# Conditioning weights of the first feed-forward asked for in threes from ScalarE, and the last layer's first weight sums for gate and up made at the end of attention

## The chip, the core and the metric

The kernel runs on one core of one Trainium2 chip. The core's engines each work through a queue of their own in order: TensorE (PE; its weight loads are shown as PEld), VectorE (DVE), ScalarE (ACT), GpSimd (POOL), and SP, which only issues transfers. ScalarE and GpSimd issue transfers too, from their own queues. Engines wait for one another through semaphores. The metric is the time of one execution in microseconds, as the median of several; lower is better.

## What is computed

Two layers of a diffusion backbone over 1024 latent tokens and 256 context tokens of width 1024. The parts that matter here:

```python
def swiglu(u, w_gate, w_up, w_down):
    return (jax.nn.silu(u @ w_gate) * (u @ w_up)) @ w_down

for i in range(DEPTH):                                  # two layers
    sh1, sc1, g1, sh2, sc2, g2 = ada_mod(c, ada_w[i], ada_b[i])   # silu(c) @ ada_w[i] + ada_b[i], in six
    u_lat = modulate(rms_norm(h_lat, norm1_g[i]), sh1, sc1)
    ...
    y_lat = mixer(...)         # layer 0: Fourier and Hyena; layer 1: neighbourhood attention, then @ na_w_out
    h_lat = h_lat + g1 * y_lat
    h_lat = h_lat + g2 * swiglu(modulate(rms_norm(h_lat, norm2_g[i]), sh2, sc2),
                                ffn_w_gate[i], ffn_w_up[i], ffn_w_down[i])
    # layer 0 does the same for the context tokens, with ada_mod(c_ctx, ...)
return rms_norm(h_lat, final_g)
```

The feed-forward's inner width is 2816, 22 blocks of 128. `ada_w` of a layer is 1024 x 6144, 48 blocks of 128 columns, 512 KB each.

## The kernel before

Values are carried transposed: 128 channels on the partitions, tokens along the free axis, eight blocks for the width of 1024. Products keep the accuracy of float32 by splitting each operand into a high part (made by ScalarE) and a low part (made by VectorE, which subtracts), and adding three products: high x high, high x low, low x high.

**The feed-forward's pair loop** (`ffn`, loop over `i`, 11 turns) makes gate and up for two blocks of the inner width at a time, with Winograd's scheme of seven products of half size in place of eight. `wino_weights` reads two weight rows of 512 KB (`ws` tiles, four buffers) and makes from their halves A11, A12, A21, A22 the sums S1 to S4 on VectorE (L1959 to L1967), then splits S1 to S4 and A22 into float16 high and low halves (`split_scaled`: L1840 on ScalarE, L1841 on VectorE; an `hl` tile is the split first row A11, A12). `wino_steps` runs the products on TensorE (L1981). Four of the seven accumulate in one PSUM bank, and between them the running sum is copied out by ScalarE (`snap`, L1986), so the next product on that bank waits for the copy; VectorE adds other banks to the copies (L1995, L2005, L2010). The gate's results then go through SiLU on ScalarE (L2125, L2127), VectorE multiplies them with up's (L2082) and makes further sums (L2085 to L2088), and GpSimd writes these out for the down projection (L338). One turn is 168 matmuls (2 x 7 products of 12). The scheduler of the framework fixes each engine's order when the program is built; `follow(x)` holds an instruction behind `x` on x's engine.

Beside the products a turn of layer 0 carries three more kinds of work:

- `ada_group`: the modulation vectors that are still missing (the last sixth of layer 0, all of layer 1) are sums over rows of `ada_w` blocks: GpSimd loads a block of 512 KB into an `s4` tile (L338), and VectorE multiplies it with the conditioning vector and sums, in two halves and for up to two conditioning vectors (L565; each shows as a CUSTOM_DVE and a short READ_ACCUMULATOR). Three blocks in each turn up to the eighth, two in the last three, 30 in all; the other 26 follow in the down projection.
- `scan`: sums of the absolute values of all gate and up rows of layer 1, for their scale. ScalarE loads a row itself (L335) and sums it some steps later (L1809); four `s4` tiles go round, four rows a turn.
- `sums`: combinations of w_down rows, loaded by SP, summed by VectorE (L2042 to L2045), written out by GpSimd.

The `s4` pool has 21 buffers. In the pair loop of layer 0 two hold the conditioning vectors, 14 the split operands, four the scan; one is left for the `ada_w` block.

**The way into the second feed-forward.** Attention (layer 1) works in groups of heads; its low halves of the transposed probabilities are made at L2530. Its TensorE time is filled with steps of the output projection over the heads already done: `first_part(0)` yields one step at a time. After it come `last_part(0)`, `first_part(1)` (its weight split is L351 on ScalarE and L353 on VectorE), and between them the first operands of the feed-forward (`wino_first`, L1775 to L1778). Behind `first_part(1)` stands `drain(self.wino_pair(1, 0, 0, sums, self.G))`: S1 to S4 and A22 of the first gate pair, from four half rows in `g` tiles. Then the first two products of several pairs are begun (`wino_begin`), and `ffn` starts: `wino_second` makes the other operands (L1853 scaling and splitting on ScalarE, L1854 and L1882 to L1903 on VectorE), while the first up pair's S1 to S4 and A22, and both of the second pair's, are made from `ws` rows among them.

Of the kernel before, what the change touches and what calls it, by code (L numbers as in the profile page):

```python
# [10 lines left out]
F32 = mybir.dt.float32  # L11
F32R = mybir.dt.float32r
F16 = mybir.dt.float16
AF = mybir.ActivationFunctionType
ALU = mybir.AluOpType
AX = mybir.AxisListType.X
MUL, ADD, SUB, MAX, MIN = ALU.mult, ALU.add, ALU.subtract, ALU.max, ALU.min

P = 128
# [239 lines left out]
class Builder:  # L259
# [280 lines left out]
    def ada_group(self, l, m, conds, where):  # L540

        nc, a = self.nc, self.a

        def load(nb):
            if where == "ws":
                t = self.W("ws", "ws")
                self.ld(t, a["ada_w"][l, nb])
                return [t[:, :512], t[:, 512:]]
            t = self.mat(1024, F32) if where == "mat" else self.S4()
            (self.ld if where == "mat" else self.ldr)(t, a["ada_w"][l, nb])  # L550
            return [t[:, :512], t[:, 512:]]

        ahead = l == 0 and m < 5
        ready = [load(m * 8)] if ahead else []
        for nb in range(m * 8, m * 8 + 8):
            if not ahead or nb < m * 8 + 7:
                ready.append(load(nb + len(ready)))
            st = ready.pop(0)
            for c in reversed(conds):
                half = self.pt.tile([P, 2], F32, tag="ah", name=self.nm("ah"))  # L560
                init = self.adab[:, l * 48 + nb:l * 48 + nb + 1]
                for j in (0, 1):
                    o = st[j] if c == 0 else self.T()
                    to = self.ada[(l, c)][:, nb:nb + 1] if j else half[:, 0:1]
                    nc.vector.tensor_tensor_reduce(o, st[j], self.cond[c][j], 1.0, init, MUL, ADD, to)  # L565
                    init = to
            yield
        sl = slice(m * 8, m * 8 + 8)
        for c in conds:
            t = self.ada[(l, c)]  # L570
            if m in (1, 4):
                g = (0 if m == 1 else 2) + l
                nc.vector.scalar_tensor_tensor(t[:, sl], t[:, sl], 1.0, self.gs[:, g * 8:g * 8 + 8], op0=ADD, op1=MUL)

    def late_groups(self, ms, where):

# [1222 lines left out]
    def scan(self, key, tiles):  # L1799

        nc = self.nc
        n = len(tiles)
        sums = self.C(2 * n)
        st = [self.S4() for _ in range(4)]
        for k in range(n + 4):
            t = st[k % 4]
            with self.follow(self.last_hi):
                if k > 3:
                    nc.scalar.activation(t, t, AF.Abs, accum_out=sums[:, k - 4:k - 3])  # L1809
                if k < n:  # L1810
                    self.lda(t, tiles[k])
            yield
        self.wsc[key] = sums
# [30 lines left out]
    def wino_second(self, h, l, m, r):  # L1844

        nc = self.nc
# [4 lines left out]
        def out(key, j, src):  # L1851
            hi, lo = self.pair((key, j), l == 1 or len(self.X) < 17)
            nc.scalar.copy(hi, src)  # L1853
            los.append(nc.vector.tensor_tensor(lo, src, self.raw_part(hi), SUB).ins)  # L1854

        los = []

# [169 lines left out]
    def ffn(self, l, u, h, hs, second, after, keep=None, begun={}):  # L2027

        nc, a = self.nc, self.a
# [19 lines left out]
        todo = iter(())  # L2049
        if l == 0:  # L2050
            self.pad(self.pt, PAD_T)
        if u is not None:
            wsums = self.wsc["here"] = self.C(4 * NFB)
            for fb in range(NFB):
                wide = 3 if fb < NFB - 2 else 2
                gh, gl = self.weights(a["gate"][l, fb], wide=wide, sums=wsums[:, fb:fb + 1])
                uh, ul = self.weights(a["up"][l, fb], wide=wide, sums=wsums[:, NFB + fb:NFB + fb + 1])
                lo = self.last_lo
                ga = self.lin(gh, gl, 0, range(KB), u, (2,))[2]
                ua = self.lin(uh, ul, 0, range(KB), u, (2,))[2]  # L2060
                t = self.T()
                nc.scalar.activation(t[:, :256], ga[:, :256], AF.Silu)
                nc.vector.tensor_tensor(t[:, :256], ua[:, :256], t[:, :256], MUL)
                self.ldr(hidc[fb // 2][:, fb % 2], t[:, :256])
                if fb >= 2:
                    with self.follow(last):
                        next(second, None)
                last = lo
            self.scale_w("here", [(0, 0), (0, 1)])
            self.load_cond(act=False)  # L2070
            todo = (x for l1, m in [(0, 5)] + [(1, m) for m in range(6)]
                    for x in self.ada_group(l1, m, (0, 1) if l1 == 0 or m < 2 else (0,), "s4"))

        ahead = iter(())
        if l == 0:
# [17 lines left out]
        for i in range(NFB // 2):  # L2093
            g, up = begun.get((i, 0)), begun.get((i, 1))
            if g is None or not g.whole:
                wg = self.wino_pair(l, i, 0, g and g.w)
                w = next(wg)
                next(wg)
            if g is None:
                g = Steps(self.wino_steps(w, lambda: self.either(self.G)))  # L2100
                g.to(1)
            if prev is not None:
                prev[0].to(7)
                finish(i - 1, prev[1])
            wu = self.wino_pair(l, i, 1, up and up.w)
            w = next(wu)
            if up is None:
                up = Steps(self.wino_steps(w, lambda: self.either(self.TK)))
            if i == 0:
                for k, _ in enumerate(second):  # L2110
                    if k == 11:
                        next(wu)
            next(wu, None)
            for k in (3, 4, 5) if i == 0 and l == 1 else ():
                g.to(k)
                up.to(k)
            next(ahead, None)
            g.to(5)
            up.to(1)
# [6 lines left out]
            t = self.G()  # L2126
# [9 lines left out]
            if i == 0 and u is not None:  # L2136
                with self.follow(self.last_hi):
                    for t in self.cond:
                        for x in t:
                            nc.scalar.activation(x, x, AF.Silu)  # L2140
            for _ in range(3 if i < 8 else 2):
                next(todo, None)
        for _ in ahead:
            pass
# [448 lines left out]
    def run(self):  # L2593
        nc, a = self.nc, self.a
# [9 lines left out]
        def drain(g):  # L2604
            for _ in g:
                pass
# [162 lines left out]
        h2, o, h4 = Act(), Act(), Act()  # L2769
# [19 lines left out]
        def by_row(x):  # L2789
            return x.rearrange("p (h r c) -> p r h c", r=8, h=4)  # L2790

        def first_part(pc):
            for nb in range(KB):
                with self.follow(self.last_mul if pc and nb > 1 else None):
                    wh, wl = self.weights(a["w_out2"][nb, :, :768], 768, load=None if pc else self.ldr)
                acc = self.PQ() if pc == 0 else self.PS()
                for kb in range(6):
                    if pc == 0 and nb == 0:
                        load_o(kb, (0,), self.ld)
# [28 lines left out]
        for i, _ in enumerate(first_part(1)):  # L2828
            if i == 7:
                c = self.rms_begin(0)  # L2830
            if i == 12:
                first = self.wino_first(h2, 1, 3, self.rms_end(0, c))
            if i > 12 and i % 3 == 1:
                with self.follow(self.last_lo):
                    next(first, None)
        sums = {}
        drain(self.wino_pair(1, 0, 0, sums, self.G))
        last_part(1)
        spill(h2, hs1, (1,))

# [45 lines left out]
        c = self.rms_begin(1)  # L2886
        begun[(0, 1)] = self.wino_begin(1, 0, 1, self.TK)
        r1 = self.rms_end(1, c)
        begun[(0, 0)].w.update(sums)
        begun[(0, 0)].whole = True  # L2890
        begun[(1, 0)] = self.wino_begin(1, 1, 0, self.G, self.TK)
        begun[(1, 1)] = self.wino_begin(1, 1, 1, self.TK, self.S2)
        begun[(2, 0)] = self.wino_begin(1, 2, 0, self.G, self.S2)
# [80 lines left out]
```

## Time and profile before

| | |
|---|---|
| median of 3 runs | 2902.62 us (2897.42 to 2906.07) |
| profiled execution, own time | 2895.03 us |
| its span, first to last instruction | 2892.9 us |
| mean granted TensorE clock | 0.983 |
| pair loop of layer 0 | about 908 to 1336 us |
| attention's last groups of heads | about 2085 to 2185 us |
| way into the second feed-forward | about 2185 to 2350 us |

The profile is of one execution. A row of a group of waits reads: who waited, at which line, for whom; total us, number of waits, the longest. A row of the timeline reads: start, duration, engine, line, operation, output<-input, shapes, how many were merged, and in brackets how long the engine had been idle and what ended that. Tile names drop their numbers: `s` is any tile of the two large pools (`s4`, `s2`), `ps` and `pq` are PSUM banks, `c` constants. "SPq" and "ACTq" rows are transfers being issued.

### The profile page before, as it was taken

The page shows a single profiled execution, that of the slowest core. Times are in us where ns is not written, and L with a number is a line of the kernel's source. Part 1 is how long each engine was busy: PE and PEld are TensorE (multiplying, and loading weights), DVE is VectorE, ACT ScalarE, POOL GpSimd, SP SyncE. Part 2 cuts the span into 40 slices and gives each one's busy share as a digit, 9 for nine tenths or more (in the row PEclk, how much of TensorE's full clock was granted, in tenths as well). Part 3 has the DMA queues.
Part 4 walks back from the last instruction along what each step waited for, and adds up shares of the span by engine and source line. Part 5 has one row for each costly group of instructions (what it writes and reads, how often), then busy time and mean ns, then how long its engine had stood idle before and what let it go on. Part 6 is the DMA issues. An engine that isn't in the chain of part 4 may idle for free. (4 is left out here: it accounts for less than half of the span.)

```text
span 2892.9 us, 43698 instructions
## 1 busy us (share of the span) xinstructions
PE 2752.6 (95%) x15570; PEld 1999.5 (69%) x15570; DVE 2095.6 (72%) x3683; ACT 1430.1 (49%) x2445; POOL 543.3 (19%) x877
## 2 busy tenths in 40 slices
PE   7999788999999999999999999999999999999998
PEld 3877677788897444445888988888887444444887
DVE  5678788768686887786887526777777976775556
ACT  3434235543686443454445426777764643343434
POOL 1210234341101112113020002333221012222000
PEclk9999999999999999999999999999999999999999
DMA  7355546656655666788995435877875235665664
GB/s 261 107 163 178 166 131 196 233 174 229 227 166 193 239 228 242 248 293 292 332 308 185 158 113 147 197 184 195 190 236 199 100 131 201 228 202 195 233 193 135
DMA packets 304936, 580.42 MB, mean 201 GB/s; under 512 B 82760, under 2 KB 129546, under 8 KB 304718
## 3 DMA queue, kind: packets, MB, share of 16 engines
q1 hardware_dynamic: 234894, 367.34, 40.7%
q0 software_dynamic: 60640, 182.50, 18.4%
q10 hardware_dynamic: 9184, 27.79, 2.8%
q8 instruction: 123, 2.02, 0.3%
q14 instruction: 95, 0.78, 0.1%
HBM read 430.17 MB, written 119.80 MB: 190 GB/s over the span
## 5 line engine op out<-in xcount | busy, mean ns | idle before, releaser
L1981 PE MATMUL ps<-s,s 128*128 128x512 f16 x2280 | 520.8, 384 | 29.1 <-ACT tk L1986 18.2
L1981 PEld LDWEIGHTS <-s 128*128 128x128 f16 x2640 | 260.3, 99 | 356.4 <-issue 50.3
L347 PE MATMUL ps<-s,wh 128*128 128x256 f32 (+1 forms) x1784 | 412.8, 334 | 8.3 <-ACT wh L351 5.2
L347 PEld LDWEIGHTS ps<-s,wh 128*128 128x128 f32 x1784 | 299.9, 191 | 43.5 <-ACT wh L351 6.9
L347 PE MATMUL ps<-s,wl 128*128 128x256 f32 (+1 forms) x892 | 272.9, 332 | 4.8 <-DVE wl L353 4.8
L351 ACT CAST s<-s 128x1024 fp32r<-128x1024 f32 (+2 forms) x192 | 172.9, 926 | 210.5 <-DMA s<-d 192.5
L2175 PE MATMUL ps<-s,s 128*128 128x512 f32 (+1 forms) x1000 | 259.0, 384 | 3.4 <-DVE s L353 3.2
L347 PE MATMUL pq<-s,wh 128*128 128x512 f32 (+1 forms) x840 | 255.8, 384 | 0.8 <-DVE s L901 0.5
L353 DVE TENSOR_TENSOR s<-s,s 128x1024 fp32r<-128x1024 f32 (+2 forms) x170 | 190.7, 1154 | 78.1 <-ACT s L351 77.7
L347 PE MATMUL ps<-s,s 128*128 128x65 f16 (+4 forms) x2748 | 229.4, 235 | 18.3 <-DMA s<-tk 9.9
L338 POOL DMA_DIRECT2D d<-s x245 | 133.6, 546 | 429.0 <-DVE s L1699 86.1
L1981 PE MATMUL ps<-s,hl 128*128 128x512 f16 x924 | 212.5, 379 | 1.2 <-ACT hl L1840 1.2
L2175 PEld LDWEIGHTS ps<-s,s 128*128 128x128 f32 x1000 | 184.3, 188 | 42.2 <-DVE s L353 5.7
L353 DVE TENSOR_TENSOR wl<-ws,wh 128x1024 fp32r<-128x1024 f32 (+1 forms) x102 | 121.3, 1192 | 120.6 <-ACT wh L351 116.1
L1981 PEld LDWEIGHTS <-hl 128*128 128x128 f16 x1056 | 103.2, 98 | 125.9 <-ACT hl L1840 1.4
L351 ACT CAST wh<-ws 128x1024 fp32r<-128x1024 f32 (+1 forms) x102 | 103.5, 1017 | 169.9 <-PE ps L347 89.9
L347 PEld LDWEIGHTS ps<-s,wl 128*128 128x128 f32 x892 | 166.3, 190 | 23.4 <-DVE wl L353 6.5
L347 PEld LDWEIGHTS pq<-s,wh 128*128 128x128 f32 x840 | 149.6, 189 | 23.0 <-ACT wh L351 1.1
L347 PE MATMUL pq<-s,wl 128*128 128x512 f32 (+1 forms) x420 | 159.1, 379 | 0.0
L2175 PE MATMUL ps<-s 128*128 128x512 f32 (+1 forms) x500 | 150.0, 386 | 1.6 <-DVE g L2010 1.6
L347 PEld LDWEIGHTS ps<-s,s 128*128 128x128 f32 (+1 forms) x828 | 130.4, 193 | 25.1 <-DVE s L353 2.6
L1840 ACT ACTIVATE s<-t,c 128x512 f16<-128x512 f32 x176 | 117.3, 712 | 23.8 <-DVE t L1964 9.9
(521 smaller groups left out, 5367.0 us busy)
## 6 DMA issues: line engine op xcount, KB each, us to landing
s<-d SPq DMA_DIRECT2D x283, 256.0 KB, 4.0
d<-s POOLq DMA_DIRECT2D x229, 256.0 KB, 3.6
s<-in_down SPq DMA_DIRECT2D x150, 256.0 KB, 6.2
s<-in_ada_w POOLq DMA_DIRECT2D x64, 512.0 KB, 5.6
ws<-in_up SPq DMA_DIRECT2D x44, 512.0 KB, 4.3
ws<-in_gate SPq DMA_DIRECT2D x42, 512.0 KB, 4.0
d<-s SPq DMA_DIRECT2D x60, 256.0 KB, 2.3
d<-g POOLq DMA_DIRECT2D x56, 256.0 KB, 3.6
```

Of the source, the lines that this page charges most:

```text
L338: self.last_ldr = self.nc.gpsimd.dma_start(out, in_).ins
L347: self.last_mm = self.nc.tensor.matmul(o, l, r, start=st, stop=sp).ins
L351: self.last_hi = nc.scalar.copy(hi, src).ins
L353: self.last_lo = eng.tensor_tensor(lo, src, hi.bitcast(F32), SUB).ins
L1840: self.last_hi = self.nc.scalar.activation(hi, src, AF.Copy, scale=s).ins
L1981: nc.tensor.matmul(ps, x[:, sl], y, start=first and j == 0 and x is wh and y is xh, stop=j == 3 and x is wl, skip_group_check=True)
L2175: m = nc.tensor.matmul(acc[j][:, c0:c1], x[:, sl], y[:, xs], start=first and k == 0, stop=last and k == 2, skip_group_check=True)
```

## The change

1. `ada_group` is replaced, in the pair loop of layer 0, by `ada_stream`. It takes three `s4` tiles of its own, has ScalarE issue three loads in a row (behind the last high half, `last_hi`), and sums the three blocks behind the last low half (`last_lo`). In turn 0 loads and sums stand at the end; in turns 1 to 9 the loads stand ahead of the scan's steps and the sums at the end. 30 blocks as before; the other 26 go on as before through GpSimd.
2. `scan` has two tiles in place of four.
3. The sums S1 to S4 and A22 of the last layer's first pair, for gate and for up, are made inside `first_part(0)`, before the third and the fifth of its eight blocks, from half rows that SP loads into `s2` tiles. The gate's `drain` behind `first_part(1)` and the up's work in the first turn of `ffn` are gone.
4. In layer 1 the second pair's weights are made behind the last low half of an operand that `wino_second` has made (`last_x`).

```diff
+    def ada_stream(self, groups, n):
+
+        blocks = [(l, m, m * 8 + k, conds) for l, m, conds in groups for k in range(8)]
...
+        own = [self.S4() for _ in range(3)]
+        for k in range(0, n, 3):
+            with self.follow(self.last_hi):
+                for t, b in zip(own, blocks[k:k + 3]):
+                    self.lda(t, self.a["ada_w"][b[0], b[2]])
+            yield
+            with self.follow(self.last_lo):
+                for t, b in zip(own, blocks[k:k + 3]):
+                    step(b, t)
+            yield
+        for b in blocks[n:]:
+            t = self.S4()
+            self.ldr(t, self.a["ada_w"][b[0], b[2]])
+            step(b, t)
+            yield
@@ scan
-        st = [self.S4() for _ in range(4)]
-        for k in range(n + 4):
-            t = st[k % 4]
+        st = [self.S4() for _ in range(2)]
+        for k in range(n + 2):
+            t = st[k % 2]
             with self.follow(self.last_hi):
-                if k > 3:
-                    nc.scalar.activation(t, t, AF.Abs, accum_out=sums[:, k - 4:k - 3])
+                if k > 1:
+                    nc.scalar.activation(t, t, AF.Abs, accum_out=sums[:, k - 2:k - 1])
@@ wino_second
             los.append(nc.vector.tensor_tensor(lo, src, self.raw_part(hi), SUB).ins)
+            self.last_x = los[-1]
@@ ffn
-            todo = (x for l1, m in [(0, 5)] + [(1, m) for m in range(6)]
-                    for x in self.ada_group(l1, m, (0, 1) if l1 == 0 or m < 2 else (0,), "s4"))
+            todo = self.ada_stream([(l1, m, (0, 1) if l1 == 0 or m < 2 else (0,))
+                                    for l1, m in [(0, 5)] + [(1, m) for m in range(6)]], 30)
...
-                w = next(wg)
-                next(wg)
+                with self.follow(self.last_x if l and i == 1 else None):
+                    w = next(wg)
+                    next(wg)
...
-            wu = self.wino_pair(l, i, 1, up and up.w)
-            w = next(wu)
-            if up is None:
-                up = Steps(self.wino_steps(w, lambda: self.either(self.TK)))
+            wu = iter(())
+            if up is None or not up.whole:
+                wu = self.wino_pair(l, i, 1, up and up.w)
...
-            next(wu, None)
+            with self.follow(self.last_x if l and i == 1 else None):
+                next(wu, None)
...
+            if i and i < 10:
+                next(todo, None)
             next(ahead, None)
...
+                next(todo, None)
-            for _ in range(3 if i < 8 else 2):
+            if i < 10:
                 next(todo, None)
@@ run
+        early = {}, {}
...
                 acc = self.PQ() if pc == 0 else self.PS()
+                if pc == 0 and nb in (2, 4):
+                    drain(self.wino_pair(1, 0, nb // 2 - 1, early[nb // 2 - 1], self.S2))
...
-        sums = {}
-        drain(self.wino_pair(1, 0, 0, sums, self.G))
...
-        begun[(0, 0)].w.update(sums)
-        begun[(0, 0)].whole = True
+        for m, x in enumerate(early):
+            begun[(0, m)].w.update(x)
+            begun[(0, m)].whole = True
```

How the instructions stand at the three places that matter. The lines of the changed program are its own: L1843 is the scan's sum (L1809 before), L1874 and L1875 the high and low halves (L1840, L1841), L2021 the copies out of PSUM (L1986), L2166 the SiLU (L2125), L570 the sums over `ada_w` (L565), L2045, L2030 and L2117 are L2010, L1995 and L2082, L1994 to L2002 are L1959 to L1967, L2572 is L2530, L2551 is L2509, L2548 is L2506.

ScalarE in a middle turn of layer 0's pair loop, before: the last split of up, four sums of the scan, the four loads of its next rows.

```order
L1840 ACTIVATE s_2617_10540<-t_10531,c_9148 128x512
L1809 ACTIVATE s_2390_9235,c_9234<-s_2390_9235 128x1024
L1809 ACTIVATE s_2391_9236,c_9234<-s_2391_9236 128x1024
L1809 ACTIVATE s_2392_9237,c_9234<-s_2392_9237 128x1024
L1809 ACTIVATE s_2393_9238,c_9234<-s_2393_9238 128x1024
L335 DMA s_2390_9235<-in_gate 128x1024
L1840 ACTIVATE hl_10843<-ws_10839,c_9148 128x1024
L1986 COPY g_10584<-ps_10458 128x512
L335 DMA s_2391_9236<-in_gate 128x1024
L335 DMA s_2392_9237<-in_gate 128x1024
```

The same engine and place in the changed program:

```order
L335 DMA s_2407_9420<-in_ada_w 128x1024
L335 DMA s_2408_9421<-in_ada_w 128x1024
L335 DMA s_2409_9422<-in_ada_w 128x1024
L1843 ACTIVATE s_2390_9235,c_9234<-s_2390_9235 128x1024
L1843 ACTIVATE s_2391_9236,c_9234<-s_2391_9236 128x1024
L1874 ACTIVATE hl_11154<-ws_11150,c_9148 128x1024
L335 DMA s_2390_9235<-in_gate 128x1024
L2166 ACTIVATE s_2647_10785<-s_2647_10785,c_9143 128x512
L335 DMA s_2391_9236<-in_gate 128x1024
L1843 ACTIVATE s_2390_9235,c_9234<-s_2390_9235 128x1024
L2021 COPY g_10901<-ps_10772 128x512
```

The three weight loads now stand behind up's last split, and the scan's third sum reads a row that was asked for three rows earlier, with the gate's copy right behind it.

VectorE in a middle turn, before: the sums over one `ada_w` block, with the gate's add (L2010) among them.

```order
L565 ISA t_10421,ah_10420<-s_2587_10418,s_2361_9156,c_101 128x512
L565 ISA ah_10420 128x1
L2045 TENSOR_TENSOR s_2576_10385<-s_2576_10385,s_2575_10384 128x512
L565 ISA t_10423,c_100<-s_2587_10418,s_2361_9156,ah_10420 128x512
L565 ISA c_100 128x1
L565 ISA s_2587_10418,ah_10425<-s_2587_10418,s_2360_9153,c_101 128x512
L565 ISA ah_10425 128x1
L1959 TENSOR_TENSOR t_10435<-ws_10430 128x512
L2010 TENSOR_TENSOR g_10258<-ps_10233,g_10258 128x512
```

VectorE in the changed program, behind the last low half of up:

```order
L1875 SCALAR_TENSOR_TENSOR s_2659_10854<-t_10845,c_9148,s_2659_10854 128x512
L570 ISA t_11042,ah_11041<-s_2407_9420,s_2361_9156,c_101 128x512
L570 ISA ah_11041 128x1
L1875 SCALAR_TENSOR_TENSOR hl_11154<-ws_11150,c_9148,hl_11154 128x1024
L2117 TENSOR_TENSOR g_10640<-ps_10595,g_10640 128x512
L570 ISA t_11044,c_100<-s_2407_9420,s_2361_9156,ah_11041 128x512
L570 ISA c_100 128x1
L570 ISA s_2407_9420,ah_11046<-s_2407_9420,s_2360_9153,c_101 128x512
L570 ISA ah_11046 128x1
L570 ISA t_11050,ah_11049<-s_2408_9421,s_2361_9156,c_101 128x512
```

The blocks' sums have moved from the stretch ahead of the gate's add to the stretch behind up's splits, and the three blocks follow each other.

VectorE in attention's last groups, before: the scores of one group (L2506, L2509), then its low halves (L2530).

```order
L2506 TENSOR_REDUCE st_22638<-ps_22517 128x2
L2509 ISA bias_22518,st_22638<-ps_22524,bias_22518,st_22638 128x384
L2509 ISA st_22638 128x1
L2509 ISA bias_22518,st_22638<-ps_22527,bias_22518,st_22638 128x384
L2509 ISA st_22638 128x1
L2530 TENSOR_TENSOR s_4668_22546<-ps_22542,s_4668_22546 128x384
```

The same group in the changed program:

```order
L2551 ISA st_22640 128x1
L1994 TENSOR_TENSOR t_22493<-s_4634_22489,s_4635_22491 128x512
L1995 TENSOR_TENSOR t_22494<-t_22493,s_4632_22485 128x512
L1999 TENSOR_TENSOR t_22503<-s_4632_22485,s_4634_22489 128x512
L2002 TENSOR_TENSOR t_22504<-s_4633_22487,t_22494 128x512
L1875 SCALAR_TENSOR_TENSOR s_4638_22497<-t_22494,c_16005,s_4638_22497 128x512
L1875 SCALAR_TENSOR_TENSOR s_4639_22500<-t_22493,c_16005,s_4639_22500 128x512
L1875 SCALAR_TENSOR_TENSOR s_4642_22506<-t_22503,c_16005,s_4642_22506 128x512
L1875 SCALAR_TENSOR_TENSOR s_4643_22509<-s_4635_22491,c_16005,s_4643_22509 128x512
L1875 SCALAR_TENSOR_TENSOR s_4644_22513<-t_22504,c_16005,s_4644_22513 128x512
L2572 TENSOR_TENSOR s_4652_22548<-ps_22544,s_4652_22548 128x384
```

The gate's four sums and five low halves now stand as one block between the scores and the low halves of a group; up's nine stand the same way three groups later.

More of the change, by code (lines that the diff above doesn't have):

```diff
@@ L557, in ada_group, with ada_block, ada_done @@
                 ready.append(load(nb + len(ready)))
[L558 to L566, printed above, removed]
-            yield
+            self.ada_block(l, nb, ready.pop(0), conds)
+            yield
+        self.ada_done(l, m, conds)
+    def ada_block(self, l, nb, st, conds):
+        for c in reversed(conds):
+            half = self.pt.tile([P, 2], F32, tag="ah", name=self.nm("ah"))
+            init = self.adab[:, l * 48 + nb:l * 48 + nb + 1]
+            for j in (0, 1):
+                o = st[j] if c == 0 else self.T()
+                to = self.ada[(l, c)][:, nb:nb + 1] if j else half[:, 0:1]
+                self.nc.vector.tensor_tensor_reduce(o, st[j], self.cond[c][j], 1.0, init, MUL, ADD, to)
+                init = to
+    def ada_done(self, l, m, conds):
         sl = slice(m * 8, m * 8 + 8)
@@ L572, in ada_group, with step @@
                 g = (0 if m == 1 else 2) + l
-                nc.vector.scalar_tensor_tensor(t[:, sl], t[:, sl], 1.0, self.gs[:, g * 8:g * 8 + 8], op0=ADD, op1=MUL)
+                self.nc.vector.scalar_tensor_tensor(t[:, sl], t[:, sl], 1.0, self.gs[:, g * 8:g * 8 + 8],
+                                                    op0=ADD, op1=MUL)
+    def ada_stream(self, groups, n):
+        blocks = [(l, m, m * 8 + k, conds) for l, m, conds in groups for k in range(8)]
+        def step(b, st):
+            l, m, nb, conds = b
+            self.ada_block(l, nb, [st[:, :512], st[:, 512:]], conds)
+            if nb % 8 == 7:
+                self.ada_done(l, m, conds)
+        own = [self.S4() for _ in range(3)]
[13 more added lines that the diff above has]
+            yield
     def late_groups(self, ms, where):
@@ L2104, in ffn @@
                 finish(i - 1, prev[1])
-            wu = self.wino_pair(l, i, 1, up and up.w)
-            w = next(wu)
-            if up is None:
-                up = Steps(self.wino_steps(w, lambda: self.either(self.TK)))
+            wu = iter(())
+            if up is None or not up.whole:
+                wu = self.wino_pair(l, i, 1, up and up.w)
+                w = next(wu)
+                if up is None:
+                    up = Steps(self.wino_steps(w, lambda: self.either(self.TK)))
             if i == 0:
@@ L2111, in ffn @@
                     if k == 11:
-                        next(wu)
-            next(wu, None)
+                        next(wu, None)
+            with self.follow(self.last_x if l and i == 1 else None):
+                next(wu, None)
             for k in (3, 4, 5) if i == 0 and l == 1 else ():
```

## The prediction

> **What bounds the kernel now.** I read the shares of the span first, then the stretches of the first feed-forward's pair loop, the waits in it by engine, the timeline of one stall, and last the stretches from the end of attention into the second feed-forward.
>
> ```profile
> span 2892.9 us, 43698 instructions
> PE 2752.6 (95%) x15570; PEld 1999.5 (69%) x15570; DVE 2095.6 (72%) x3683; ACT 1430.1 (49%) x2445; POOL 543.3 (19%) x877
> ```
>
> TensorE is the bound over the whole, so time can only come from its idle 140 us and from slowed matmuls. Stretches (us; busy time and count of PE, PEld, DVE, ACT, POOL; clock; DMA share; GB/s) of the loop's start, of six whole turns in its middle, and of the next turn and a half:
>
> ```profile
> 908.00:987.00 79.00, 73.37 (x337) 32.85 (x338) 61.66 (x115) 35.89 (x59) 11.77 (x22) 0.99 0.64 221
> 987.00:1232.00 245.00, 227.11 (x1008) 100.41 (x1008) 199.49 (x375) 109.03 (x180) 46.23 (x87) 0.97 0.69 241
> 1232.00:1291.00 59.00, 57.74 (x260) 25.78 (x260) 56.02 (x99) 33.99 (x56) 12.49 (x23) 0.97 0.83 293
> ```
>
> The waits of VectorE and of TensorE in those six turns, and of ScalarE there:
>
> ```profile
> DVE t L565 <- DMA s<-in_ada_w: 44.8, 12, 5.4
> PE ps L1981 <- ACT tk L1986: 14.4, 6, 3.2
> PE ps L1981 <- DVE s L2005: 4.0, 5, 1.4
> ACT g L2125 <- DVE g L2010: 50.5, 6, 9.1
> ```
>
> VectorE's 199.5 us of work and its 44.8 us of waiting for conditioning weights make 244.3 of 245. So in these turns the bound is not TensorE: VectorE has no other free time, and the rest queues behind it. One stall shows how (VectorE, ScalarE, TensorE, and a shorter stall with what follows it):
>
> ```profile
> 1063.29 0.75 DVE L565 CUSTOM_DVE_ANT_0 t<-s,s,c 128x512 f32<-128x512 f32 x1 [2.46 <-DMA s<-in_ada_w]
> ...
> 1066.52 0.69 DVE L2010 TENSOR_TENSOR g<-ps,g 128x512 f32<-128x512 f32 x1
> 1067.24 0.72 ACT L2125 ACTIVATE g<-g,c 128x512 f32<-128x512 f32 x1 [8.79 <-DVE g L2010]
> 1067.87 0.57 ACT L1986 COPY tk<-ps 128x512 f32<-128x512 f32 x1
> 1028.12 10.52 PE L1981 MATMUL ps<-s,s 128*128 128x512 f16 x48 [1.80 <-ACT tk L1986]
> 1038.48 5.34 PE L1981 MATMUL ps<-s,hl 128*128 128x512 f16 x24
> ...
> 1068.49 11.98 PE L1981 MATMUL ps<-s,s 128*128 128x512 f16 x48 [2.79 <-ACT tk L1986]
> 1080.30 5.34 PE L1981 MATMUL ps<-s,hl 128*128 128x512 f16 x24
> ```
>
> The late weight block delays the add at L2010, the SiLU at L2125 waits for the add, the copy at L1986 stands behind the SiLU, and TensorE may not accumulate on that bank before the copy. Full pace is (1038.48 - 1028.12) / 48 = 0.216 us a matmul; after the stall of 2.79 us the same 48 took 11.81 us, 1.45 more. Six turns are 1008 matmuls, 217.6 us at that pace, so 27.4 us of the 245 are lost: 17.9 idle (245 - 227.1) and 9.5 slow.
>
> [...]
>
> **Why the weights come late, and the loop after.** GpSimd's queue, its row over the whole loop, and the loop's loads to landing (KB each, median us; last, least, median and most for the loads of gate rows):
>
> ```profile
> POOL s L338 <- DVE c L565: 103.0, 22, 20.7
> s<-in_ada_w POOLq DMA_DIRECT2D x33, 512.0 KB, 4.3
> s<-in_gate ACTq DMA_DIRECT2D x22, 512.0 KB, 7.4
> DMA to landing us min/median/max: 3.4/4.7/10.4
> ```
>
> GpSimd waits for VectorE to free the one buffer (22 times), then the load takes 4.3 us, with VectorE in front of an empty buffer: two of the three loads of a turn show as waits, 12 x 3.7 us. The change asks for three buffers at once, right after the up splits, and sums them behind the same splits. Work stays: 33.2 us of VectorE a turn (199.5 / 6), against TensorE's 36.3 (217.6 / 6). What decides is X, the wait for the first of three; the sums of one block cover the next. How early ScalarE gives out a load in its queue:
>
> ```profile
> 1083.25 0.82 ACTq L335 DMA_DIRECT2D s<-in_gate  x2
> 1083.89 1.14 ACT L1840 ACTIVATE hl<-ws,c 128x1024 f16<-128x1024 f32 x1
> 1084.93 0.56 ACT L1986 COPY g<-ps 128x512 f32<-128x512 f32 x1
> ```
>
> These loads stand behind both the split and the copy in ScalarE's order, and went out 1.7 us before the copy began. VectorE reaches its first sum about two of its operations (1.3 us) after the last split, so the lead is 1.3 + 1.7 = 3.0 us and X = 4.3 - 3.0 = 1.3. Ends: 0, if the queue runs further ahead; 7.4 - 1.3 = 6.1, if it doesn't and the three land as the bursts on ScalarE's queue do. I take 1.3, from the row of the same bytes. VectorE's turn is then 34.5 us, under TensorE's 36.3, which becomes the bound; I keep the other wait of TensorE (L2005, 4.0 / 6 = 0.7): 37.0 a turn in place of 40.8. Six turns give 23 us. At the loop's start 5.6 us are idle, and I take 3, the size of one such stall. From 1232 to 1291 TensorE is busy 57.7 of 59: nothing. **Loop: -26**, between -9 (X = 6.1: 39.3 a turn, 1.5 x 6) and -33 (27.4 + 5.6).
>
> Thirty triggers of 0.33 us join ScalarE, busy under half of these turns (109 of 245): nothing, while no load blocks it (second rival). GpSimd loses 30 triggers and its long waits; the writes behind them leave earlier, and no wait of TensorE above is for one of them: nothing. SP now asks for a gate row ahead of the four pieces of w_down; those only feed sums that are written out for a later stage: nothing.
>
> **Attention's end and the second feed-forward.** Stretches; VectorE's rows ahead of the projection's stall, and TensorE's row of it; a row of attention; and a wait of TensorE between 2280 and 2310:
>
> ```profile
> 2140.00:2160.00 20.00, 20.00 (x192) 17.89 (x191) 14.69 (x33) 12.92 (x31) 4.70 (x9) 1.00 0.60 191
> 2160.00:2180.00 20.00, 20.00 (x217) 17.41 (x215) 13.10 (x29) 12.85 (x33) 3.83 (x7) 1.00 0.65 205
> 2220.00:2240.00 20.00, 17.27 (x66) 13.09 (x65) 17.28 (x26) 9.57 (x16) 0.00 (x0) 0.91 0.48 154
> 2280.00:2300.00 20.00, 17.37 (x78) 7.30 (x77) 20.00 (x32) 12.47 (x21) 0.00 (x0) 1.00 0.17 53
> 2300.00:2320.00 20.00, 18.16 (x76) 7.63 (x75) 20.00 (x32) 13.61 (x22) 0.00 (x0) 0.91 0.26 79
> 2214.49 0.69 DVE L1960 TENSOR_TENSOR t<-t,g 128x512 f32<-128x512 f32 x1
> 2215.10 0.69 DVE L1964 TENSOR_TENSOR t<-g,g 128x512 f32<-128x512 f32 x1
> ...
> 2230.83 0.74 DVE L1841 SCALAR_TENSOR_TENSOR s<-t,c,s 128x512 f16<-128x512 f32 x1
> 2231.49 0.74 DVE L1841 SCALAR_TENSOR_TENSOR s<-g,c,s 128x512 f16<-128x512 f32 x1
> 2232.15 0.74 DVE L1841 SCALAR_TENSOR_TENSOR s<-t,c,s 128x512 f16<-128x512 f32 x1
> ...
> 2233.48 0.95 DVE L353 TENSOR_TENSOR wl<-ws,wh 128x768 fp32r<-128x768 f32 x1
> 2234.48 0.50 PE L347 MATMUL ps<-s,wl 128*128 128x512 f32 x1 [2.46 <-DVE wl L353]
> 2147.53 0.56 DVE L2530 TENSOR_TENSOR s<-ps,s 128x384 f16<-128x384 f32 x1 [1.24 <-ACT s L2529]
> PE ps L1981 <- DVE s L1841: 1.5, 1, 1.5
> ```
>
> The gate's five low halves (L1841) stand right before the split that TensorE waits 2.46 us for, and the clock of that stretch is 0.91 (1.8 us of 20). They go to attention: **-4.3**, between 0 (the first-row products that move up take their place) and -4.5.
>
> In the second feed-forward VectorE is busy without a gap from 2280 to 2320 while TensorE idles 2.6 + 1.8 us and the clock costs 1.8. The up sums leave this place: four adds of 0.60 and five low halves of 0.66 (start to start in the rows above), 5.7 us; the second pair's weights now queue behind the operand splits, so what VectorE makes first is what TensorE takes first. **-4.5** of 6.2: the 1.5 us that end with a weight's low half, the 1.8 of the clock, and 1.2 of the other 2.9, since waits for the operands themselves can stay; between 0 and -6.2.
>
> The price lies in attention: 5.7 us of VectorE twice, as one block in front of the low halves at L2530, where it idled 1.24 us. In those stretches it idles 5.3 and 6.9 us, TensorE none, having projection steps to fill with. **+2**, between 0 (the fill covers) and +9 (each block shows, less 1.24). The ten ScalarE splits, 0.6 us each, stand between the exponentials and are in these bounds.
>
> Sum: -26 - 4.3 - 4.5 + 2 = -32.8 on the profiled execution's 2895.0 us, so 2862; its time is 7.6 below the runs' median of 2902.6, hence 2870 there.
>
> **Rivals.** (1) The bytes set the pace: three 512 KB loads in a burst share the engines with everything else, X is 6.1 and VectorE still waits: loop -9, sum -15.8, 2887. For it: ScalarE's bursts land at 7.4 us; against it: the first of a burst lands before the median, and the share is 0.69. [...]
>
> (2) Slower: the weight scan has two buffers, so in each turn ScalarE meets a sum over a tile that it asked for only three rows before, and behind it stands the copy of the gate's bank, which that gate's next product there needs. ScalarE's scan and splits:
>
> ```profile
> 1068.52 1.95 ACT L1840 ACTIVATE s<-t,c 128x512 f16<-128x512 f32 x3
> 1079.73 1.04 ACT L1809 ACTIVATE s<-s 128x1024 f32<-128x1024 f32 x1
> ```
>
> In the new order that product stands 85 matmuls (18.4 us) behind the up product whose copy opens ScalarE's run; two copies (0.57 each), five splits (0.65), a sum (1.04) and the trigger's own 0.33 put the trigger 5.8 us behind it. Less the waiting sum (1.04) and the copy (0.57) the landing may take 11.0 us; the longest seen is 10.4, the median 7.4. Each us more costs ten turns 1 us each, so 33 us are gone at 14.3; at 15 the kernel takes 2902.6 - 32.8 + 40 = 2910. For it: these loads now queue behind 1.5 MB of weights; against: 3.6 us of margin over the median landing.
>
> (3) Attention pays in full and the second feed-forward gains nothing: -26 - 4.3 + 9 = -21.3, 2881. For it: TensorE waits on L2530 earlier in attention; against: the fill, which kept TensorE at 20.0 of 20 there.
>
> (4) The slow stretches do not come from the stalls and stay, as a clock lowered by something else would make them: the loop gives 17.9 idle less 4.0 kept, plus 3, so -17, and the sum is -24, 2879. Against it: the two stalls shown above, one with full pace behind it and one without. [...]
>
> **How the numbers follow.** Forecast 0.58; rival 1 0.20, 2 0.05, 3 0.12, 4 0.05. Under 0.3% (8.7 us; the three runs spread by as much) a change can't be told from none. Rival 1 with more waits or 3 with less gain falls within it: 0.04 + 0.02. Faster 0.89, same 0.06, slower 0.05. The range takes all lower ends (-33 - 4.5 - 6.2 gives 2859, and 6 for the spread), and above it rival 1 with part of 3: 2853 to 2893; what it leaves out is rival 2 and the weak ends of 1 and 3.
>
> **What would show it.** In the new profile six turns should take 222 us with VectorE's wait for in_ada_w under 8 us, from one load a turn; the clock there 1.00; the wait of 2.46 us on L353 gone; TensorE idle under 2 us between the first operands and the second pair. Wrong, if that wait is still 30 us or more, if TensorE waits on copies behind ScalarE's absolute sums, or if L2530 appears among TensorE's waits with over 5 us in attention's last 60 us.

## The result, and the profile after

Seven runs of the changed kernel have a median of 2871.9 us (2859.6 to 2880.5), seven of the kernel before beside them 2899.2 (2886.5 to 2914.4). The ratio of the runs is 0.9892, 95% interval 0.9860 to 0.9925: 31 us faster (27 by the medians), where 33 were forecast. A second set, timed later beside two of the experiments, gave 0.9921 (0.9895 to 0.9946). The profiled execution took 2874.6 us.

The page of the changed kernel, its span and its engines:

```profile
span 2872.7 us, 43713 instructions
PE 2746.6 (96%) x15570; PEld 2004.2 (70%) x15570; DVE 2093.1 (73%) x3683; ACT 1435.3 (50%) x2445; POOL 527.0 (18%) x847
```

VectorE's work is the same to 2.5 us and TensorE's busy time fell by only 6.0; idle time went. Both kernels run 15570 matmuls in nearly the same order, so a stage can be taken from the start of the same matmul, by its number, in each profile. The loop's start, the six turns and the next turn and a half (columns as before):

```profile
912.00:989.10 77.10, 74.72 (x337) 33.30 (x338) 70.64 (x129) 44.62 (x72) 8.70 (x16) 0.98 0.68 241
989.10:1207.50 218.40, 217.54 (x1009) 98.55 (x1008) 194.05 (x370) 110.06 (x179) 34.55 (x64) 1.00 0.75 262
1207.50:1263.90 56.40, 56.21 (x261) 25.41 (x260) 49.29 (x88) 30.85 (x50) 9.38 (x18) 1.00 0.81 298
```

The six turns take 218.4 us in place of 245, at clock 1.00, with TensorE idle for 0.9: they are at the 217.6 that 1008 matmuls take at 0.216 us each. The waits of VectorE, TensorE and ScalarE there:

```profile
ACT s L1843 <- DMA s<-in_gate: 26.3, 6, 8.0
...
DVE hl L1875 <- ACT hl L1874: 18.2, 6, 3.8
...
ACT s L1843 <- DMA s<-in_up: 15.3, 3, 7.7
...
DVE t L570 <- DMA s<-in_ada_w: 3.8, 4, 1.4
...
PE ps L2016 <- ACT g L2021: 0.9, 1, 0.9
```

VectorE's 44.8 us of waiting for conditioning weights are 3.8; it now waits 18.2 for ScalarE's splits of the first rows, which costs nothing here. ScalarE itself waits 41.6 us for the scan's rows (its two tiles), and the only wait that TensorE shows is 0.9 us for a copy. Attention's end (797 matmuls), a part of the out-projection, and the 151 matmuls where the second feed-forward had stalled; then TensorE's waits in the first of the three, and the longest that it had in the whole of attention before, other than for DMA:

```profile
2079.90:2173.70 93.80, 81.60 (x799) 70.90 (x798) 69.76 (x148) 59.75 (x136) 16.89 (x31) 0.95 0.65 197
2210.30:2225.70 15.40, 15.12 (x66) 11.96 (x65) 13.79 (x21) 6.77 (x10) 0.00 (x0) 1.00 0.38 133
2265.70:2299.30 33.60, 32.97 (x153) 14.79 (x152) 33.60 (x55) 21.47 (x36) 1.08 (x2) 1.00 0.13 46
```

```profile
PE ps L347 <- ACT t L2553: 5.7, 1, 5.7
...
PE ps L2568 <- ACT t L2553: 4.2, 2, 2.4
```

```profile
PE ps L347 <- DVE s L2530: 1.7, 2, 1.0
PE ps L347 <- ACT t L2511: 1.2, 1, 1.2
```

The same matmuls took 81.8, 19.9 and 39.9 us before. The last two are faster, but attention's end is 12.0 us longer, the largest loss anywhere. The stages, in us of each profile (the names are those of the experiments below):

| matmuls | before | whole change | loop_only | end_only | spread | scan2_only | scan2_spread |
|---|---|---|---|---|---|---|---|
| loop's start | 78.8 | 77.1 | 74.5 | 79.1 | 77.4 | 73.8 | 73.7 |
| six turns | 245.0 | 218.4 | 217.8 | 244.6 | 217.3 | 217.8 | 217.3 |
| next 260 | 58.9 | 56.4 | 56.8 | 60.9 | 56.1 | 56.1 | 56.1 |
| loop's end, down projection's start | 88.8 | 91.2 | 91.4 | 90.3 | 91.9 | 91.0 | 93.2 |
| attention's end | 81.8 | 93.8 | 83.4 | 88.1 | 86.1 | 84.5 | 85.9 |
| out-projection (200) | 55.0 | 52.0 | 55.1 | 51.4 | 50.6 | 56.0 | 49.3 |
| second feed-forward's start | 39.9 | 33.5 | 39.9 | 33.5 | 33.5 | 38.2 | 33.8 |

What is left are stretches that no part of the change touches: up to matmul 4606 the profiles spread from 903 to 913 us, and attention ahead of its end (matmuls 8700 to 11650) from 313 to 322, in no order that follows the edits. Single totals differ by 10 us for that reason. Half clock is in these times too: a slow stretch costs about half its length (1.45 us behind the stall of 2.79 us in before, where the recorded clock was 0.50 for 3.41 us), and attention's end holds none of it in before and scan2_spread, 3.4 us in loop_only, end_only, spread and scan2_only, and 10.2 in the whole change.

### The profile page after: what moved, and what is told of

It is laid out like the page before. It is cut to its first block, busy times and chain, and to the rows that moved or that the text cites. A ratio compares the mean times of both kernels' runs of the same rounds, so it can differ in the third digit from the quotient of the medians.

```text
span 2872.7 us, 43713 instructions
## 1 busy us (share of the span) xinstructions
PE 2746.6 (96%) x15570; PEld 2004.2 (70%) x15570; DVE 2093.1 (73%) x3683; ACT 1435.3 (50%) x2445; POOL 527.0 (18%) x847
## 5 line engine op out<-in xcount | busy, mean ns | idle before, releaser
L2016 PE MATMUL ps<-s,s 128*128 128x512 f16 x2280 | 511.8, 380 | 5.5 <-ACT g L2021 5.3
L353 DVE TENSOR_TENSOR s<-s,s 128x1024 fp32r<-128x1024 f32 (+2 forms) x170 | 190.5, 1153 | 78.8 <-ACT s L351 78.6
L353 DVE TENSOR_TENSOR wl<-ws,wh 128x1024 fp32r<-128x1024 f32 (+1 forms) x102 | 121.2, 1191 | 120.6 <-ACT wh L351 116.2
L1875 DVE SCALAR_TENSOR_TENSOR s<-t,c,s 128x512 f16<-128x512 f32 x176 | 128.3, 743 | 6.8 <-ACT s L1874 6.7
```

The costliest lines, as they stand in the source:

```text
L353: self.last_lo = eng.tensor_tensor(lo, src, hi.bitcast(F32), SUB).ins
L1875: self.last_lo = self.nc.vector.scalar_tensor_tensor(lo, src, s, hi, op0=MUL, op1=SUB).ins
L2016: nc.tensor.matmul(ps, x[:, sl], y, start=first and j == 0 and x is wh and y is xh, stop=j == 3 and x is wl, skip_group_check=True)
```

## The experiments

**Each part alone.** `loop_only` has parts 1 and 2 of the change, `end_only` parts 3 and 4.

```diff
 loop_only, from the changed kernel:
-                if pc == 0 and nb in (2, 4):
-                    drain(self.wino_pair(1, 0, nb // 2 - 1, early[nb // 2 - 1], self.S2))
...
+        sums = {}
+        drain(self.wino_pair(1, 0, 0, sums, self.G))      # behind first_part(1)
...
-            with self.follow(self.last_x if l and i == 1 else None):
...
 end_only: ada_group and four scan tiles as before
```

> The loop's part of the change alone (three blocks asked for at once by ScalarE, two scan tiles); the first pair's sums stay where they were before. Theory A (read from the two profiled executions, matmul by matmul: the loop gives 28 us, the out-projection and the second feed-forward give 11, and attention's end takes about 13 back): 28 us faster than before, so within 5 us of the whole change, and TensorE has no wait on the exponentials (L2553) of over 1.5 us in attention's last 60 us. Theory B (the prediction's terms: loop -26, the rest -7): 26 us faster, 5 to 7 us slower than the whole change.

> The other part alone: the first pair's sums for gate and up inside attention and the second pair behind last_x; the loop as before. Theory A: the 11 us gained behind attention are given back in it, so between 3 us faster and 4 us slower than before; TensorE waits for the exponentials (4 to 6 us in two waits behind the two blocks). Theory B: 7 us faster, with at most 2 us more idle time of TensorE in attention.

Measured: loop_only 0.9907 (0.9885 to 0.9930), 27 us faster, level with the whole change; end_only 0.9997 (0.9982 to 1.0013), nothing. The six turns of loop_only, and waits there; then, of end_only, VectorE's wait in its six turns with TensorE's in attention's end (the exponentials are L2516 there), and that stage:

```profile
987.60:1205.40 217.80, 217.73 (x1009) 98.50 (x1008) 195.68 (x372) 110.03 (x178) 35.14 (x66) 1.00 0.75 267
```

```profile
ACT s L1843 <- DMA s<-in_gate: 27.5, 6, 7.6
...
ACT s L1843 <- DMA s<-in_up: 13.7, 3, 7.5
...
DVE t L570 <- DMA s<-in_ada_w: 2.9, 3, 1.6
```

```profile
DVE t L565 <- DMA s<-in_ada_w: 44.4, 12, 5.3
...
PE ps L2531 <- ACT t L2516: 4.2, 2, 2.4
```

```profile
2104.00:2192.20 88.20, 80.62 (x799) 69.47 (x798) 69.82 (x148) 59.70 (x136) 16.85 (x31) 0.98 0.67 208
```

With the loop's part alone VectorE's wait is down to 2.9 us; with the other alone it stands as before, and TensorE waits 4.2 us for exponentials. So the loop carries the whole gain, and the other part gains behind attention what it loses in it, as theory A had both.

**Who issues, or how many buffers.** `scan2_only` is the kernel before with two scan tiles; GpSimd loads block by block as it did.

```diff
-        st = [self.S4() for _ in range(4)]
+        st = [self.S4() for _ in range(2)]
...
```

> Before, with two scan tiles in place of four and nothing else: GpSimd still issues the loads of conditioning weights, one by one, but three buffers are free for them, so it can ask up to three blocks ahead. Theory A (the gain in the loop comes from the buffers; who issues is of no account): 20 to 28 us faster, VectorE waits under 10 us for in_ada_w in six turns. Rival D (the loads must come as a burst at the right point, from a queue with no waiting writes in it: GpSimd's queue holds them behind its writes): under 15 us faster, and VectorE still waits over 20 us in six turns.

Measured: 0.9882 (0.9861 to 0.9903), 34 us faster, more than the 20 to 28 expected, with the scan's number of tiles alone changed and no load moved to ScalarE. Its six turns take 217.8 us too. ScalarE's and VectorE's waits in them (the sums are L565, the scan L1809), then its loads of conditioning weights in the loop (KB, median us to landing), and the same row of loop_only:

```profile
ACT s L1809 <- DMA s<-in_gate: 8.2, 6, 2.6
...
ACT s L1809 <- DMA s<-in_up: 4.7, 4, 2.6
...
DVE s L565 <- DMA s<-in_ada_w: 1.6, 1, 1.6
```

```profile
s<-in_ada_w POOLq DMA_DIRECT2D x32, 512.0 KB, 5.3
```

```profile
s<-in_ada_w ACTq DMA_DIRECT2D x30, 512.0 KB, 8.3
```

The buffers are the mechanism. Asked for one at a time, the blocks land sooner (5.3 us against 8.3) and the scan's rows are waited for 12.9 us (8.2 + 4.7) in place of loop_only's 41.2. Issued by ScalarE in threes, the blocks landed no earlier.

`scan3_only` leaves three tiles to the scan, so two buffers for the blocks; `scan1` is the whole change with one scan tile, which puts the second rival to the test.

> Before, with three scan tiles: two buffers are free for the conditioning weights. Theory A (one buffer more is enough: while one block is summed, 2.7 us, the next is already there, and only the third of a turn is asked for late): VectorE waits 1 to 3 us a turn for in_ada_w, its turn stays under TensorE's 36.3, and the loop gains as much as with three buffers within 4 us. Rival F (three are needed): VectorE's waits stay over 4 us a turn and the six turns take over 225 us.

> The whole change with one scan tile in place of two: each row is asked for only when the row before it is summed, so ScalarE meets each sum a full landing (5 to 8 us) after its load whenever two steps stand next to each other. The prediction's second rival says what follows: copies stand behind the waiting sum, and TensorE waits for them; with 4 sums a turn waiting 5 us or more ScalarE, busy 18 us a turn, passes 36.3, so the ten turns take 20 to 100 us longer than in the whole change and TensorE waits over 15 us for copies at L2021 in six turns. If the copies have room for this too: no change.

Measured: scan3_only 0.9925 (0.9907 to 0.9943), 22 us faster. Its six turns, and the waits there:

```profile
986.20:1210.70 224.50, 218.32 (x1009) 98.34 (x1008) 199.66 (x385) 108.36 (x177) 46.55 (x86) 1.00 0.76 266
```

```profile
PE ps L1981 <- ACT s L1986: 4.4, 5, 1.3
...
DVE s L565 <- DMA s<-in_ada_w: 2.4, 1, 2.4
...
DVE t L565 <- DMA s<-in_ada_w: 1.7, 2, 1.5
```

Both expectations missed: VectorE waits only 4.1 us, yet TensorE idles 6.2, in stalls of at most 1.7 us, and the clock stays at 1.00. Two buffers give 20.5 of the 27 us of these turns. That VectorE's order still brings some copies late is the likely reason for the rest; it was not taken apart.

Measured: scan1 0.9923 (0.9902 to 0.9944), 7 us over the first timing of the whole change by the medians, and level with its second (0.9921), where 20 to 100 us were expected. Its six turns and ScalarE's waits:

```profile
987.50:1204.80 217.30, 217.30 (x1008) 98.52 (x1007) 198.18 (x376) 112.63 (x181) 35.69 (x66) 1.00 0.77 269
```

```profile
ACT s L1843 <- DMA s<-in_gate: 34.5, 11, 5.4
...
ACT s L1843 <- DMA s<-in_up: 19.4, 7, 4.7
```

ScalarE waits 53.9 us, 9 a turn and not the 20 expected, and TensorE none: 112.6 of work and 53.9 of waiting still fit into 217.3. What its profile shows as a cost lies behind the turns (98.2 us at the loop's end against 91.2). The second rival's mechanism is not there at half its buffers.

**The block in attention.** The end of attention in the changed kernel: VectorE's adds of the gate's first sums, ScalarE's splits, the exponentials, and TensorE; ahead of it the wait that ended at 2089.79:

```profile
2088.49 0.51 ACT L2434 ACTIVATE s<-t,c 128x256 f16<-128x256 f32 x1 [8.29 <-DMA t<-d]
...
2127.88 0.69 DVE L1995 TENSOR_TENSOR t<-t,s 128x512 f32<-128x512 f32 x1
...
2128.66 1.33 ACT L1874 ACTIVATE s<-t,c 128x512 f16<-128x512 f32 x2 [0.77 <-DVE t L1995]
...
2129.90 1.55 ACT L2553 ACTIVATE t<-ps,st 128x256 f32<-128x256 f32 x4
2130.41 0.44 PE L2568 MATMUL ps<-c,t 128*128 128x128 f32 x2 [2.40 <-ACT t L2553]
```

ScalarE waits for the add, splits twice, and only then makes the four exponentials that TensorE needs next. The wait of 5.7 us stands 38 us ahead of the first block, behind a load; at that place the other profiles, with blocks and without, show waits from under 0.7 to 4.1 us (4.0 in scan2_only, which leaves attention as it was, and 2.2 in whole_again, the same kernel once more), so it is not the change's. `spread` hands the same work out one sum and one split at a time:

```diff
-                if pc == 0 and nb in (2, 4):
-                    drain(self.wino_pair(1, 0, nb // 2 - 1, early[nb // 2 - 1], self.S2))
...
+            op("A22", a22)
+            yield
+            nc.vector.tensor_tensor(a22, a21, a22, ADD)
+            op("S1", a22)
+            yield
...
+                    if pc == 0 and nb and kb % 3 == 1:
+                        next(pieces, None)
```

> The whole change, but the ten splits and eight sums of the first pair are handed out one at a time, one sum with its split at every third step of the output projection in attention, made in place, in place of two blocks of nine. Theory A (the price in attention comes from VectorE's and ScalarE's blocks, which stand in front of the exponentials): attention takes at most 4 us more than before in place of 13, and the time falls 8 to 10 us below the whole change, to about 36 us under before. Rival C (the price is the transfers: 2 MB more of weight rows in attention's end, or the order of its loads): the time stays within 3 us of the whole change.

Measured: 0.9868 (0.9841 to 0.9896), 36 us under before, as theory A had it; the whole change stands at 0.9892 and 0.9921, and the intervals overlap. The same rows of weights are loaded there, so their bytes alone are not the price that rival C took them for. TensorE's waits of 2.4 and 1.8 us are gone from attention's end, and the longest left is the one behind the load:

```profile
PE ps L347 <- ACT t L2553: 2.5, 1, 2.5
...
PE ps L347 <- DVE s L2572: 1.0, 1, 1.0
```

Attention's end, over all kernels: without the first sums 81.8, 83.4, 84.5 and 82.1 us (mean 83.0); with blocks 93.8, 88.1, 91.1, 89.6 and 92.5 (91.0); handed out 86.1, 85.9, 87.8 and 83.4 (85.8). So blocks cost 5 us more than single pieces, and the pieces 3. Slow clock is in these means: with half of each slow stretch taken off they are 82.1, 87.6 and 84.5, so of the 8 us the order takes 3, the work 2.5 and the clock 2.5, part of it behind the load that has nothing to do with the change.

**Both together, and last_x.** `scan2_spread` joins the two; `no_last_x` takes the fourth part of the change from it.

```diff
 no_last_x, from scan2_spread:
-                with self.follow(self.last_x if l and i == 1 else None):
-                    w = next(wg)
-                    next(wg)
+                w = next(wg)
+                next(wg)
...
-            with self.follow(self.last_x if l and i == 1 else None):
-                next(wu, None)
+            next(wu, None)
```

> Two scan tiles with GpSimd's loads as they were (scan2_only), and the first pair's sums handed out one by one in attention (spread), with the second pair behind last_x. If the two gains add: scan2_only -34 and spread -36.5 against loop_only -27 give 34 + 9.5 = 43 us under before, 2856. If scan2_only's 7 us over loop_only are chance (both took 217.8 us for the six turns in their profiles): 36 under before, 2863, level with spread.

> scan2_spread without the fourth part of the change: the second pair's weights are not held behind last_x. Theory A (the 6.3 us at the start of the second feed-forward come from the up sums that are gone, 5.7 us of VectorE): the same time as scan2_spread within 2 us, and the 151 matmuls behind the first 12826 take at most 35 us. Rival E (the order does it: what VectorE makes first is what TensorE takes first): 3 to 6 us slower than scan2_spread, and TensorE waits there again for low halves of weights.

Measured: scan2_spread 0.9845 (0.9825 to 0.9865), median 2855.6 us, the fastest kernel here and 45 us under before, where 43 were expected if the two gains add; no_last_x 0.9868 (0.9848 to 0.9888), slower by 7 us in the medians, with intervals that overlap. The second feed-forward's start in scan2_spread, in no_last_x and in loop_only, and TensorE's longest wait there in no_last_x:

```profile
2246.10:2279.90 33.80, 32.90 (x153) 14.77 (x152) 33.80 (x55) 21.59 (x36) 1.09 (x2) 1.00 0.14 46
```

```profile
2253.90:2291.30 37.40, 34.47 (x153) 15.08 (x152) 37.40 (x60) 25.75 (x42) 0.00 (x0) 0.95 0.17 57
```

```profile
2261.70:2301.50 39.80, 35.34 (x152) 14.90 (x151) 39.80 (x63) 26.07 (x43) 0.00 (x0) 0.96 0.21 66
```

```profile
PE pq L1982 <- ACT g L1987: 1.8, 1, 1.8
```

Without last_x the stage takes 37.4 us, over the 35 of theory A. Such times have to be compared at the same clock: 3.4 us of these 37.4 ran at half clock, as in before and loop_only, which still make up's sums there and take 39.9. The two other kernels with these sums, scan2_only and scan3_only, have the same waits at full clock and take 38.2. So the sums that are gone give 2.5 of the stage's 6.1 us (39.9 to 37.4), and the order 3.6 (37.4 to 33.8), 1.7 of them by the clock. The wait for a weight's low half that rival E expected is not among those of no_last_x; its longest is for a copy.

**The issuer once more.** `whole_gpsimd` is the whole change with GpSimd's loads, `whole_again` the changed kernel beside it, `spread_first` is spread with the first three blocks loaded by GpSimd ahead of the loop (its first `next(todo)` stands there).

```diff
 spread_first, from spread:
-            with self.follow(self.last_hi):
+            with self.follow(self.last_hi if k else None):
...
-                    self.lda(t, self.a["ada_w"][b[0], b[2]])
+                    (self.lda if k else self.ldr)(t, self.a["ada_w"][b[0], b[2]])
...
+            next(todo)
...
-                next(todo, None)
```

> The whole change, blocks in attention included, but the loads of conditioning weights stay with GpSimd, one by one, as in scan2_only. Against whole_again beside it. Theory G (who issues matters: ScalarE asks late in the first turn and its bursts of 1.5 MB delay the scan's rows): 3 to 8 us faster than whole_again, and the loop's start (337 matmuls from number 4606) takes 74 us in place of 77. Rival H (the earlier difference of 7 us between the kernels with GpSimd's and with ScalarE's loads was chance): within 2 us of whole_again.

> The changed kernel itself, beside the other two of this call: 27 to 31 us faster than before, as measured first; the two waits of 2.4 and 1.8 us for the exponentials stand behind its two blocks again, and the wait of 5.7 us that stood ahead of them in the first profile is shorter, as it was in every other kernel.

> spread with one thing more: the three blocks of the first turn are loaded by GpSimd ahead of the loop, the others by ScalarE in threes as in the change. If the loop's start explains why ScalarE's loads are slower than GpSimd's: the loop's start takes 74 us in place of 77 and the time is about 3 us under spread, 39 to 40 under before. If it is the bursts inside the loop or chance: 36 to 37 under before, and the start stays at 77.

Measured: 0.9894 (0.9875 to 0.9912), 0.9921 (0.9895 to 0.9946) and 0.9870 (0.9851 to 0.9889). whole_again is 21 us under before by the medians, less than expected. The loop's start in the three, in that order, and VectorE's wait in the second:

```profile
913.20:986.40 73.20, 72.96 (x338) 32.96 (x339) 67.19 (x123) 43.73 (x71) 12.40 (x23) 1.00 0.75 261
```

```profile
912.50:990.00 77.50, 74.41 (x337) 33.20 (x338) 70.76 (x129) 44.65 (x71) 8.67 (x16) 0.98 0.68 240
```

```profile
DVE t L570 <- DMA s<-in_ada_w: 2.8, 1, 2.8
```

```profile
908.80:982.60 73.80, 73.09 (x338) 32.89 (x339) 70.23 (x128) 44.71 (x72) 8.12 (x15) 1.00 0.67 229
```

In the first turn ScalarE asks late: 4 us of the loop's start, which the three early loads remove. Over the whole kernel they hardly show: spread_first is level with spread in the ratios (0.9870 and 0.9868) and 2 us ahead of it in the medians, each against its own kernel before, which is between the two values expected. Whether ScalarE's loads cost anything more stays open: in each of three pairs the kernel with GpSimd's is the faster, by 0.2 to 0.3%, but the intervals overlap, and whole_gpsimd is level with the first timing of the whole change (0.9892).

## Why the prediction was right, and where it was not

The total came out (2870 against 2871.9), the sum behind it only in part: the second part was to bring 6.8 us and brings about nothing, and the loop brings more than forecast. That these nearly cancel is luck.

- **Loop: -26 forecast, -28.4 measured.** Start -1.7 (forecast -3), six turns -26.6 (-23, since 4.0 us of TensorE's waits were kept that are now 0.9), the next 260 matmuls -2.5 (nothing), and 2.4 more at the loop's end. Slow clock is 1.7 of these 2.4, and end_only, whose scan still has four tiles, takes 90.3 us there, so the loss is not shown to be the smaller scan's. The mechanism held: loads one at a time into one buffer were the bound, and with them gone TensorE is.
- **X: 1.3 us a turn forecast, 0.6 measured (3.8 / 6), by two errors that cancel.** ScalarE's split, its first load, up's last high half, up's last low half and the first sum, in one turn of the changed kernel, and the loads' median to landing in the loop:

```profile
1059.77 0.73 ACT L1874 ACTIVATE s<-t,c 128x512 f16<-128x512 f32 x1
1059.88 0.35 ACTq L335 DMA_DIRECT2D s<-in_ada_w  x1
...
1062.23 0.71 ACT L1874 ACTIVATE s<-t,c 128x512 f16<-128x512 f32 x1
...
1066.07 0.74 DVE L1875 SCALAR_TENSOR_TENSOR s<-t,c,s 128x512 f16<-128x512 f32 x1
...
1068.25 0.75 DVE L570 CUSTOM_DVE_ANT_0 t<-s,s,c 128x512 f32<-128x512 f32 x1 [1.43 <-DMA s<-in_ada_w]
```

```profile
s<-in_ada_w ACTq DMA_DIRECT2D x30, 512.0 KB, 8.2
```

  The load stands behind the last split in ScalarE's order and went out 2.4 us before that split began. The lead was 8.4 us here, 6.3 to 8.4 over the turns, not 3.0; the landing 8.2 in the median, not 4.3. Taking the duration from GpSimd's lone loads for a burst of three was the error that rival 1 named; the lead saved it.
- **Attention: +2 forecast, +12.0 in the profile, +8.0 over the kernels with blocks.** This is the step that failed. "Projection steps to fill with" was the reason for the low value, but TensorE took no step from behind a late exponential in its place: it idled 2.40 us to 2130.41 and 1.79 to 2153.33, and the next steps, which stand behind in its order, ran from 2133.39 and 2155.05. These two waits are 4.2 us; slow clock is the next part (0.98 of end_only's 88.2 us, 1.8). The wait was looked for at L2572, behind VectorE's block; it came one operation earlier, at the exponentials, through ScalarE's splits, which had no term of their own in the sum.
- **Out-projection: -4.3 forecast, -3.0 here and -3.6 over the kernels with blocks** (means of 55.3 and 51.7). The wait of 2.46 us at L353 is gone and one slow stretch of two with it, but in this profile another wait on the same line, 118 matmuls earlier, has grown from 0.2 us:

```profile
PE ps L347 <- DVE wl L353: 1.5, 1, 1.5
```

- **Second feed-forward: -4.5 forecast, -6.4 measured**, the full bound. TensorE idles 0.6 us there. By no_last_x the order gives 3.6 us of this and the sums that are gone 2.5.
- **Rivals.** 1: its landing was right (8.2 us, forecast 7.4), its wait was not. 2: with half the scan's buffers, in scan1, TensorE still doesn't wait. 3: the first half came true (8 of 9 us), the second did not. 4: the clock is 1.00 in the six turns, so the slow stretches did come from the stalls. Its sum of -24 was 3.6 too large, since -4.3 and -4.5 hold 1.8 of clock each that would have stayed.

By these stages the second part of the change sums to +8.0 - 3.6 - 5.5 = -1.1 us over the kernels with and without it, and end_only's interval (5 us faster to 4 slower) holds that; forecast was -6.8.

## What to carry to other kernels

When an engine waits for loads into one buffer, count the buffers ahead of the queues: here taking two from a neighbour that could spare them did all that re-issuing from another engine did (34 us, against 27 with the loads re-issued too). Work that moves off a critical place goes into an in-order queue elsewhere: give it there one piece at a time, since a block of nine stands in front of whatever that stage needs next (here 2.40 and 1.79 us of TensorE's time). A sum that comes out right can hide two terms that were wrong; only kernels with one part each show it.

## What the runs showed of the hardware

The prediction's rows show a stall of 2.79 us with slow matmuls behind it and one of 1.80 us with full pace. A stall's length alone doesn't decide. In the kernel before the recorded clock was 0.50 from 1068.06 to 1071.47, behind the stall of 2.79 us; it was 1.00 from 1944 to 1960, though TensorE stood idle for 2.82 us to 1947.05; and it was 0.50 from 2214.94 to 2218.35, beginning in a stall of 1.54 us. In the changed kernel a stall of 1.78 us that ended at 1314.44 was followed by 0.50 (1314.96 to 1318.37), and one of 1.79 us that ended at 2153.33 by 1.00 (to 2160).

Between 800 and 2835 us the record has ten slow stretches in the profile of before and seven in that of the changed kernel, each at 0.50 and 3.41 or 6.83 us long. Each begins during a stall of TensorE of 1.36 us or more, or within 1.7 us of the end of one. What else decides was not shown.
